# Issuing the adaLN weight rows of a hybrid layer from ScalarE's queue

## The chip, the cores and the metric

The kernel runs on one core of a Trainium2 chip. The core has five engines with instruction streams of their own: TensorE (PE, and PEld for its weight loads), VectorE (DVE), ScalarE (ACT), GpSimd (POOL) and the sync engine (SP). An engine takes its instructions in a fixed order; DMAs are instructions too, and occupy the queue of the engine that issues them, which first waits until the buffer to be filled is free. The transfer itself is done by 16 DMA engines that all queues share. The metric is the device time of one execution in microseconds.

## The reference

One layer works on x of 256 x 2048 (S = 256 positions) with a conditioning vector c of 2048, all in fp32:

```python
def _layer(x, c, w_ada, b_ada, ...):
    ada = (jax.nn.silu(c) @ w_ada + b_ada)[:, None, :]
    sh1, sc1, g1, sh2, sc2, g2, sh3, sc3, g3 = jnp.split(ada, N_ADA, axis=-1)
    h = _swiglu(_modulate(x, sh1, sc1), ffn1_w_in, ffn1_w_out)
    x = _layernorm(ALPHA * x + 0.5 * (1 + g1) * h, ln1_g, ln1_b)
    h = _token_mixer(_modulate(x, sh2, sc2), w_in, ..., w_out)
    x = _layernorm(ALPHA * x + (1 + g2) * h, ln2_g, ln2_b)
    h = _swiglu(_modulate(x, sh3, sc3), ffn2_w_in, ffn2_w_out)
    x = _layernorm(ALPHA * x + 0.5 * (1 + g3) * h, ln3_g, ln3_b)
    return x
```

The two feed-forward parts go from 2048 to 2 x 5632 and back. The token mixer has 8 attention heads with forget gates and 4 mLSTM heads. `w_ada` has 2048 x 18432 numbers, 151 MB, all used once, for a single vector: the product `silu(c) @ w_ada` gives nine vectors of 2048 features.

## The kernel before, in words

**Weights.** Every product with x or h has fp32 accuracy from three products of rounded numbers: high times high, low times high, high times low (`mm3`, L444 to L447). A weight tile of 1 MB (512 x 512) is loaded by SP into one of three buffers `raw` (`load_w`, L406); each half is then cast to its high part by ScalarE (L155) and its low part is the difference, taken by VectorE (L156). There are six buffers each for high and low parts, that is, three tiles. TensorE passes 24 products of 128 x 128 over 512 columns for a tile. A weight tile can be loaded as soon as the low part of the tile three before is taken.

**The ada rows.** The product with `w_ada` is done on VectorE: a row is a block of 128 x 1024 numbers (512 KB), and `acc += row * silu(c)` (L168 for the first row, L170 for the others) sums 16 of them into `acc` (or into part of `gate`), followed by a small TensorE product over the partitions that gives columns or gates. There are 288 such rows. Two buffers (`araw`) hold them: a row is asked for one ahead (`ask`, L188 to L192), so that its load waits until the sum of the row two earlier is done.

**Which rows, and when.** `AdaQueue` deals rows out to the weight tiles at a fixed rate (`R_F` 1.25 rows per tile in the first feed-forward part, 1.12 to 1.27 in the next ones, 1 and 0.7 in the last). The stages, with the times of the profile: the first features of x (shift and scale of the first norm, 512 features at a time) at the beginning, up to about 230 us, together with the first products (tiles `s`); the remainder of the first feed-forward input (`f1i`, 290 to 520), its output (`f1o`, to 760), the mixer (to 1160), the second feed-forward part (`gu`, `fh`, `f2i`, `f2o`, to the end). Rows last until 1500 us.

**The first features** are handled apart: the first 512 (`first_ada0`, L923) by 16 rows loaded by SP; the others (`first_ada(j)` for j = 1 to 3, L945 to L970) by 48 rows, three buffers (two `araw` and one `aw`), three of them on SP and 45 on GpSimd. After the last row of each, `first_columns` takes the columns (`cp`, L854; `scsh`, L856), which the next products need.

**The order.** The framework that turns the program into instruction streams has a planner of its own: it estimates times and sets the order on each engine by readiness and priority, so that a row's load stands in the queue where the planner puts it, not where it is written. At the changes of stage the order on VectorE and ScalarE is written out by hand. `tc.issue_after(ins)` keeps what is traced in its block behind `ins`, for instructions on the same engine as `ins`. One such block is in `load_mixer_smalls`, where three small loads wait behind the last row of `first_ada`:

```python
with tc.issue_after(pin_rows[0]):
    G_.dma_start(gbias[:, 0:8], fox_f_bias[0:1, :].to_broadcast([P, 8]))
    G_.dma_start(gbias[:, 8:12], mlstm_i_bias[0:1, :].to_broadcast([P, 4]))
    G_.dma_start(gbias[:, 12:16], mlstm_f_bias[0:1, :].to_broadcast([P, 4]))
```

In the code `SP`, `G_`, `S`, `V` and `PE` are the sync engine, GpSimd, ScalarE, VectorE and TensorE.

Of the kernel before, what the change touches and what calls it, by code (L numbers as in the profile page):

```python
# [14 lines left out]
P = 128  # L15
# [17 lines left out]
def layer_kernel(  # L33
# [8 lines left out]
    V, S, G_, PE, SP = nc.vector, nc.scalar, nc.gpsimd, nc.tensor, nc.sync  # L42
# [99 lines left out]
    pin_rows = [None]  # L142
# [20 lines left out]
    def pair_cols(v, j):  # L163
        return w_ada[0, :, v * D:(v + 2) * D].rearrange("k (v n) -> k v n", v=2)[:, :, j * 512:(j + 1) * 512]

    def ada_acc(acc, raw, k):
        if k == 0:
            V.tensor_scalar_mul(acc, raw, csil[:, k:k + 1])  # L168
        else:
            V.scalar_tensor_tensor(out=acc, in0=raw, scalar=csil[:, k:k + 1], in1=acc,  # L170
                                   op0=ALU.mult, op1=ALU.add)
# [14 lines left out]
    wanted, asked = [], []  # L186

    def ask():  # L188
        if wanted:
            shape, src, tag, k = wanted.pop(0)  # L190
            asked.append(ap.tile(shape, F32, tag="araw", bufs=2, name=f"ar{tag}_{k}"))
            SP.dma_start(asked[-1], src[k * P:(k + 1) * P])  # L192

    def ada_rows(acc):
        for k in range(KD):
            if not asked:
                ask()
            ada_acc(acc, asked.pop(0), k)
            ask()
            yield  # L200
# [140 lines left out]
    def modulate_both(v, j, rs, xT):  # L341
        xf = npool.tile([P, 4, T], F32, tag="xf", name=f"xf{ntag()}")
        n = xf.rearrange("p k t -> p (k t)").rearrange("p (a n) -> p a n", a=2)
        for a in range(2):
            S.activation(n[:, a, :], res[:, a, j * 512:(j + 1) * 512], AF.Identity, bias=rs[a][:, 1:2],
                         scale=rs[a][:, 0:1])
        yield
        tps = [aux_tile(f"tp{ntag()}") for _ in range(2)]
        for q in range(4):
            for a in range(2):  # L350
                PE.transpose(tps[q // 2][:, (2 * (q % 2) + a) * P:(2 * (q % 2) + a + 1) * P],
                             n[:, a, q * P:(q + 1) * P], ident)
        yield
        for q in range(4):
            k = 4 * j + q
            S.activation(xf[:, q, :], tps[q // 2][:, (q % 2) * T:(q % 2 + 1) * T], AF.Identity,
                         bias=scsh[:, v, k:k + 1], scale=scsh[:, v + 1, k:k + 1])
            hi, lo = (x[:, k, :] for x in xT[:2])
            cast = S.copy(hi, xf[:, q, :])  # L359
            yield  # L360
            x_cast[0] = cast.ins
            pin["x"] = V.tensor_tensor(out=lo, in0=xf[:, q, :], in1=hi.bitcast(F32), op=ALU.subtract).ins
            yield
# [483 lines left out]
    def first_columns(j, acc, mb):  # L847
        cps = aux_tile(f"cp{j}"), mm_tile(f"cq{j}")

        def column(q):  # L850
            cp = cps[q % 2][:, q:q + 2]
            qs = slice(q * P, (q + 1) * P)
            for v in range(2):
                PE.matmul(cp[:, v:v + 1], acc[:, v, qs], ones[:, 0:1], start=True, stop=True)  # L854
            k = 4 * j + q
            V.tensor_tensor(out=scsh[:, 0:2, k:k + 1], in0=cp.unsqueeze(2), in1=bcol[:, 0:2, k:k + 1], op=ALU.add)  # L856

        column(0)
        next(mb)
        column(1)  # L860
        next(mb)
        next(mb)
        column(2)
        next(mb)
        column(3)
        next(mb)
        for _ in mb:
            pass
# [77 lines left out]
    def first_ada(j):  # L946
        src = pair_cols(0, j)
        if j % 2:
            acc = ap.tile([P, 2, 512], F32, tag="acc", name=f"acc0_{j}")
        else:  # L950
            acc = gate[:, :1024].rearrange("p (v n) -> p v n", v=2)
        for k in range(KD):
            where, tag, n = (ep, "aw", 1) if k % 3 == 2 else (ap, "araw", 2)
            raw = where.tile([P, 2, 512], F32, tag=tag, bufs=n, name=f"ar0_{j}_{k}")
            pin_rows[0] = (SP if j == 1 and k < 3 else G_).dma_start(raw, src[k * P:(k + 1) * P]).ins
            if k < KD - 1:
                ada_acc(acc, raw, k)
            else:
                for b in range(2):
                    bs = slice(b * 256, (b + 1) * 256)  # L960
                    ada_acc(acc[:, :, bs], raw[:, :, bs], k)
            if k == 11:
                mb = modulate_both(0, j, rs0, xT)
            if k in (11, 13):
                next(mb)
            yield
        first_columns(j, acc, mb)
        yield
# [138 lines left out]
    for j in range(4):  # L1107
        fa = first_ada(j + 1) if j < 3 else load_mixer_smalls()
        for i in range(NS):
            with ExitStack() as s:  # L1110
                if j == 0 and i in (1, 2):

                    s.enter_context(tc.issue_after(x_cast[0]))
                    s.enter_context(tc.issue_after(pin["x"]))
                first_in(j, i, ws if i + j == 0 else first_w(j, i))
            for _ in range((2 * (j > 0), 1 + 2 * (j == 0), 2, 1, 2, 2, 1, 2, 1, 2, 1, 0)[i] if j < 3
                           else i not in (4, 9, 11)):
                with pinned():
                    next(fa, 0)
            if j == 3 and i > 2:  # L1120
                pump(R_F)
# [692 lines left out]
```

## Time and profile before

| | |
|---|---|
| three runs | 1854.41, 1858.54, 1861.12 us |
| median | 1858.54 us |
| profiled execution | 1855.95 us, span of the instructions 1854.2 us |
| TensorE busy | 1820.5 us of the span |
| VectorE busy | 1452.9 us |
| ScalarE busy | 926.3 us |
| GpSimd busy | 61.7 us |
| mean granted TensorE clock | 0.997 of full speed |
| transferred | 510.44 MB, mean 275 GB/s |

The profile names each group by source line, engine, operation and tile. PEld is the loading of the stationary operand, which overlaps the products. A letter q behind an engine (SPq, ACTq) is its sequencer, where waits for semaphores and DMA issues take place; these are not counted as busy time. In lists of waits the three numbers are total, times and longest.

### The profile page before, as it was taken

Reading aid. Unit: us, or ns where it says so; the run is one execution under the profiler, and the core shown is the slowest. Engines: PE = TensorE matmul, PEld = TensorE weight load, DVE = VectorE, ACT = ScalarE, POOL = GpSimd, SP = SyncE. Lnnn points to the kernel's source line nnn. Section 1 sums busy time; section 2 is a strip of 40 time slices with the busy share of each in tenths; the row PEclk is TensorE's granted clock in tenths of the full one; section 3 lists DMA queues with packets and bytes.
Section 4 is the critical chain, followed back from the end, with each engine's and each line's share of the span. In section 5 each row is a group of like instructions: output and inputs, shape, how many; then the busy total and the mean of one; then the engine's idle time right before and its main releaser. Section 6 shows DMA issues by size and latency. Waiting matters only on the chain.

```text
span 1854.2 us, 25052 instructions
## 1 busy us (share of the span) xinstructions
PE 1820.5 (98%) x9577; PEld 1599.3 (86%) x9577; DVE 1452.9 (78%) x1787; ACT 926.3 (50%) x1332; POOL 61.7 (3%) x92
## 2 busy tenths in 40 slices
PE   7999999999999999999999999999999999999997
PEld 4888888888888888699999887888889999988887
DVE  6889989877787787788889888787997766564655
ACT  3554455443554344755666645555465444554441
POOL 1211100000000000000000000000000000000000
PEclk9999999999999999999999999999999999999999
DMA  9989978988988898489979883998877876666663
GB/s 364 379 293 328 328 231 304 328 308 299 312 294 276 304 305 315 151 295 320 325 264 307 327 298 117 326 347 287 303 255 254 274 233 201 205 204 201 203 202 144
DMA packets 242927, 510.44 MB, mean 275 GB/s; under 512 B 10834, under 2 KB 52466, under 8 KB 241784
## 3 DMA queue, kind: packets, MB, share of 16 engines
q1 hardware_dynamic: 234696, 477.90, 74.7%
q0 software_dynamic: 8112, 30.95, 4.8%
q8 instruction: 75, 1.23, 0.3%
q14 instruction: 44, 0.36, 0.0%
HBM read 506.71 MB, written 2.10 MB: 274 GB/s over the span
## 4 chain that ended last, share of the span: by engine, by line
PE 56%; DVE 1%; issue 1%; ACT 0%; DMA 0%; POOL 0%; DVEq 0%; ACTq 0%; POOLq 0%; SPq 0%
PE gu_f L450 8%; PE o_f L446 4%; PE o_f L445 4%; PE o_f L447 4%; PE gu_f L451 4%; PE fh L446 4%; PE fh L447 4%; PE fh L445 4%; PE o_mx L445 1%; PE o_mx L446 1%; PE o_mx L447 1%; PE b_mv L445 1%; PE b_fv L445 1%; PE pr_m L445 1%; PE b_mv L446 1%; PE b_fv L446 1%
## 5 line engine op out<-in xcount | busy, mean ns | idle before, releaser
L170 DVE SCALAR_TENSOR_TENSOR acc<-ar,csil,acc 128x1024 f32<-128x1024 f32 (+1 forms) x167 | 211.7, 1269 | 65.8 <-DMA ar<-in_w_ada_dram 65.4
L450 PE MATMUL gu_f<-x_f,hi_f2i 128*128 128x512 f32 x640 | 210.0, 382 | 0.0
L451 PE MATMUL gu_f<-x_f,lo_f2i 128*128 128x256 f32 x640 | 174.5, 273 | 0.0
L156 DVE TENSOR_TENSOR lo_f2o<-raw_f2o,hi_f2o 128x1024 fp32r<-128x1024 f32 x86 | 105.2, 1224 | 86.7 <-ACT hi_f2o L155 86.6
L155 ACT CAST hi_s<-raw_s 128x1024 fp32r<-128x1024 f32 x96 | 99.1, 1047 | 117.4 <-PE s L447 64.8
L155 ACT CAST hi_f1o<-raw_f1o 128x1024 fp32r<-128x1024 f32 x86 | 88.4, 1047 | 120.6 <-PE o_f L447 63.3
L155 ACT CAST hi_f2o<-raw_f2o 128x1024 fp32r<-128x1024 f32 x86 | 90.1, 1047 | 115.6 <-PE o_f L447 107.0
L446 PE MATMUL s<-lo_s,x_f 128*128 128x512 f32 x384 | 146.2, 381 | 1.2 <-DVE lo_s L156 1.1
L445 PE MATMUL s<-hi_s,x_f 128*128 128x512 f32 x384 | 146.4, 383 | 0.2 <-ACT x_f L359 0.2
L447 PE MATMUL s<-hi_s,x_f 128*128 128x512 f32 x384 | 145.5, 379 | 0.0
L156 DVE TENSOR_TENSOR lo_f2i<-raw_f2i,hi_f2i 128x1024 fp32r<-128x1024 f32 x80 | 97.9, 1224 | 54.2 <-ACT hi_f2i L155 53.7
L450 PEld LDWEIGHTS gu_f<-x_f,hi_f2i 128*128 128x128 f32 x640 | 121.0, 189 | 16.8
L445 PE MATMUL o_f<-hi_f1o,hi 128*128 128x512 f32 x344 | 131.4, 382 | 3.1 <-DVE hT L1021 2.0
L447 PE MATMUL o_f<-hi_f1o,lo 128*128 128x512 f32 x344 | 131.0, 381 | 0.0
L446 PE MATMUL o_f<-lo_f1o,hi 128*128 128x512 f32 x344 | 131.0, 381 | 0.0
L155 ACT CAST hi_f1i<-raw_f1i 128x1024 fp32r<-128x1024 f32 x80 | 81.1, 1045 | 99.4 <-DMA raw_f1i<-in_ffn_w_in_dram 71.8
L170 DVE SCALAR_TENSOR_TENSOR gate<-ar,csil,gate 128x1024 f32<-128x1024 f32 (+1 forms) x94 | 117.5, 1251 | 16.3 <-DMA ar<-in_w_ada_dram 15.9
L156 DVE TENSOR_TENSOR lo_s<-raw_s,hi_s 128x1024 fp32r<-128x1024 f32 x96 | 115.9, 1220 | 14.8 <-ACT hi_s L155 14.8
L445 PE MATMUL o_f<-hi_f2o,hi 128*128 128x512 f32 x332 | 125.8, 379 | 0.0
L446 PE MATMUL o_f<-lo_f2o,hi 128*128 128x512 f32 x332 | 125.8, 379 | 0.0
L447 PE MATMUL o_f<-hi_f2o,lo 128*128 128x512 f32 x332 | 125.8, 379 | 0.0
L155 ACT CAST hi_fh<-raw_fh 128x1024 fp32r<-128x1024 f32 x80 | 82.4, 1048 | 81.3 <-DMA raw_fh<-in_ffn_w_in_dram 37.0
(447 smaller groups left out, 4830.7 us busy)
## 6 DMA issues: line engine op xcount, KB each, us to landing
ar<-in_w_ada_dram SPq DMA_DIRECT2D x230, 512.0 KB, 5.5
raw_s<-in_ffn_w_in_dram SPq DMA_DIRECT2D x47, 1024.0 KB, 7.6
raw_f1o<-in_ffn_w_out_dram SPq DMA_DIRECT2D x44, 1024.0 KB, 7.3
raw_f2o<-in_ffn_w_out_dram SPq DMA_DIRECT2D x44, 1024.0 KB, 5.0
raw_f1i<-in_ffn_w_in_dram SPq DMA_DIRECT2D x40, 1024.0 KB, 7.5
raw_fh<-in_ffn_w_in_dram SPq DMA_DIRECT2D x40, 1024.0 KB, 7.4
raw_f2i<-in_ffn_w_in_dram SPq DMA_DIRECT2D x40, 1024.0 KB, 5.8
ar<-in_w_ada_dram POOLq DMA_DIRECT2D x45, 512.0 KB, 6.3
```

The lines of the kernel that those rows point to most:

```text
L155: S.copy(hi, src)
L156: return V.tensor_tensor(out=lo, in0=src, in1=hi.bitcast(F32), op=ALU.subtract)
L170: V.scalar_tensor_tensor(out=acc, in0=raw, scalar=csil[:, k:k + 1], in1=acc, op0=ALU.mult, op1=ALU.add)
L445: PE.matmul(o, ah, bh, start=start, stop=False)
L446: PE.matmul(o, ah, bl, start=False, stop=False)
L447: PE.matmul(o, al, bh, start=False, stop=stop)
L450: PE.matmul(o, ah, x.rearrange("p s (a n) -> p s n a", a=2), start=start, stop=False)
L451: PE.matmul(o[:, T:], al, woven(x[:, 0]), start=False, stop=stop)
```

## The change

Two lines. The rows that `ask` loads (224 in the trace) go from SP's queue to ScalarE's, and the 45 rows of `first_ada` that GpSimd loaded do so too. The first 16 rows (`first_ada0`) and the three of j = 1 remain on SP. Nothing else is edited: buffers, rates and sums are the same.

```diff
@@ ask
             shape, src, tag, k = wanted.pop(0)
             asked.append(ap.tile(shape, F32, tag="araw", bufs=2, name=f"ar{tag}_{k}"))
-            SP.dma_start(asked[-1], src[k * P:(k + 1) * P])
+            S.dma_start(asked[-1], src[k * P:(k + 1) * P])
@@ first_ada
             where, tag, n = (ep, "aw", 1) if k % 3 == 2 else (ap, "araw", 2)
             raw = where.tile([P, 2, 512], F32, tag=tag, bufs=n, name=f"ar0_{j}_{k}")
-            pin_rows[0] = (SP if j == 1 and k < 3 else G_).dma_start(raw, src[k * P:(k + 1) * P]).ins
+            pin_rows[0] = (SP if j == 1 and k < 3 else S).dma_start(raw, src[k * P:(k + 1) * P]).ins
```

## The prediction

> **What bounds the kernel now.** I read the busy times first, then the table by stretches of time, then the waits, the sync engine's own waits, and last the timeline of the one stage in which the row loads touch the critical path. The time of the profiled execution is 1855.95 us for a span of 1854.2, 2.6 us below the median of the three runs (1858.54); the sum below is made against 1855.95, and 2.6 is added to compare with medians.
>
> ```profile
> PE 1820.5 (98%) x9577; PEld 1599.3 (86%) x9577; DVE 1452.9 (78%) x1787; ACT 926.3 (50%) x1332; POOL 61.7 (3%) x92
> ...
> 0.00:40.00 40.00, 29.30 (x110) 16.84 (x111) 24.02 (x55) 10.26 (x16) 2.81 (x11) 1.00 0.98 360
> 40.00:100.00 60.00, 56.94 (x272) 48.53 (x270) 48.16 (x45) 37.38 (x52) 11.77 (x16) 1.00 1.01 372
> 100.00:160.00 60.00, 60.00 (x286) 52.65 (x285) 55.53 (x62) 27.57 (x33) 10.14 (x14) 1.00 0.87 306
> 160.00:230.00 70.00, 69.06 (x335) 60.24 (x334) 67.05 (x80) 31.64 (x36) 13.60 (x20) 1.00 0.94 324
> ...
> 290.00:520.00 230.00, 228.34 (x1083) 199.22 (x1082) 179.15 (x172) 101.13 (x130) 1.08 (x2) 1.00 0.89 310
> 520.00:760.00 240.00, 235.93 (x1085) 204.32 (x1084) 192.78 (x217) 107.44 (x129) 3.34 (x5) 0.99 0.82 287
> 850.00:1060.00 210.00, 209.91 (x1590) 200.54 (x1589) 185.45 (x291) 130.00 (x249) 3.78 (x3) 1.00 0.88 305
> 1160.00:1310.00 150.00, 150.00 (x700) 131.31 (x699) 120.17 (x120) 82.14 (x105) 0.58 (x1) 1.00 0.91 319
> ```
>
> The columns after the length are busy PE, PEld, DVE, ACT and POOL, then the granted clock, the DMA share and GB/s. TensorE is the bound: 98% of the span. In the stretches in which rows are loaded it stands still 3.06 us (40 to 100), 0.94 (160 to 230), 1.66 (290 to 520) and 4.07 (520 to 760), together 9.73; in 850 to 1060 and 1160 to 1310 it hardly does (0.09 and 0.00). Nothing that is done to row loads can gain more than about these 9.73 us; what they can lose has no such limit. What ended those stops:
>
> ```profile
> PE o_f L445 <- DVE hT L1021: 2.0, 1, 2.0
> PE cp L854 <- DVE scsh L856: 1.9, 1, 1.9
> PE gu_f L446 <- DVE lo_f1i L156: 1.2, 2, 0.7
> PE o_f L445 <- DVE res L556: 1.1, 1, 1.1
> PE s L446 <- DVE lo_s L156: 1.1, 2, 0.8
> ```
>
> (Total, times, longest.) The low parts of weights (lo_f1i, lo_s) and the column product cp are late by a microsecond here and there; hT and res belong to the change of stage at 521 and 639 us and wait for no row.
>
> **The change part by part.** 224 rows of 512 KB go from SP to ScalarE (L192) and 45 from GpSimd to ScalarE (L955). The two buffers for rows, the order of the sums on VectorE and the bytes stay.
>
> ```profile
> L192 SPq DMA_DIRECT2D ar<-in_w_ada_dram x224: 327/367/500, 220.6 to 1499.1; - x112
> L955 POOL DMA_DIRECT2D ar<-in_w_ada_dram x45: 714/724/889, 43.0 to 217.4; - x45
> SPq L192 <- DVE acc L170: 233.3, 125, 7.0
> SPq L192 <- DMA ar<-in_w_ada_dram: 146.0, 90, 3.5
> SPq L192 <- DVE gate L170: 129.9, 64, 7.7
> ```
>
> *Issue time.* 269 x 0.37 = 99.5 us of ScalarE's queue, if an issue costs there what it costs on SP. ScalarE is busy 926.3 of 1854.2 us, so it has room: in 290 to 520, 50 rows take 18.5 of the 128.9 us it stands idle. By itself I take 0 for this; its cover is the lead of the casts over TensorE. Saved: 45 x 0.72 us on GpSimd, which nothing waits for, and 224 x 0.37 = 82 us on SP.
>
> *The waits.* Here lies the risk. On SP the row's issue waits for its buffer: 233.3 + 146.0 + 129.9 = 509 us over 224 rows, 2.3 us each, with only weight tiles behind it, which have three buffers. On ScalarE the same waiting instruction has casts (L155) behind it, and behind a cast VectorE's low part and TensorE. How much of the 2.3 us moves along depends on where the row will stand in ScalarE's order. Ends: nothing (the row stands where its buffer is free) and all of it. The stage of f1i, where ScalarE, VectorE and the row loads all wait:
>
> ```profile
> SPq L192 <- DVE acc L170: 45.8, 29, 4.8
> SPq L192 <- DMA ar<-in_w_ada_dram: 44.6, 28, 3.5
> SPq L192 <- DVE gate L170: 28.5, 15, 5.8
> ...
> ACT hi_f1i L155 <- DMA raw_f1i<-in_ffn_w_in_dram: 71.8, 24, 6.1
> DVE acc L170 <- DMA ar<-in_w_ada_dram: 21.1, 18, 2.8
> ...
> 419.77 5.68 SPq L192 DMA_DIRECT2D ar<-in_w_ada_dram  x2
> 425.54 0.42 SPq L406 DMA_DIRECT2D raw_f1i<-in_ffn_w_in_dram  x1
> ...
> 421.12 1.99 ACT L155 CAST hi_f1i<-raw_f1i 128x1024 fp32r<-128x1024 f32 x2 [5.51 <-DMA raw_f1i<-in_ffn_w_in_dram]
> ...
> 423.76 1.28 DVE L170 SCALAR_TENSOR_TENSOR acc<-ar,csil,acc 128x1024 f32<-128x1024 f32 x1 [1.75 <-DMA ar<-in_w_ada_dram]
> ...
> 462.22 0.62 ACT L155 CAST ahi<-acc 128x512 fp32r<-128x512 f32 x1 [8.45 <-DVE acc L170]
> ...
> 462.33 0.38 PE L445 MATMUL gu_f<-hi_f1i,x_f 128*128 128x512 f32 x1
> 463.38 0.48 PE L446 MATMUL gu_f<-lo_f1i,x_f 128*128 128x512 f32 x1 [0.67 <-DVE lo_f1i L156]
> ```
>
> (The first three are SP's waits in 290 to 520, the next two waits of the same stretch.) At 419.77 two rows hold SP until the second is issued just ahead of 425.45, and only then goes the weight tile out; ScalarE in turn waits 5.51 and then, from the same view, again for weights. That speaks for the change: a tile that leaves SP without a row ahead of it lands earlier. The last three rows price the danger: ScalarE, held 8.45 us for a sum on VectorE (from 453.77, two casts before it), leaves TensorE a step of 463.38 - 462.33 = 1.05 us instead of the 0.21 between neighbours (228.34 / 1083), 0.84 us lost. So a single hold costs TensorE what goes beyond about 7.6 us, and the short holds of a row (longest on SP here 5.8) cost nothing by themselves, only by adding up. What adds up: SP's whole wait would be 45.8 + 44.6 + 28.5 = 118.9 us, and with 18.5 of issue 137.4 against ScalarE's idle 128.9, 8.5 too much; the break-even is (128.9 - 18.5) / 50 = 2.2 us a row. I take the middle, about 1.2 us a row, since ScalarE reaches a row only after a cast that itself waits (24 of them waited 3 us each for weights) and finds the buffer freer than SP did: no loss from the adding up. Against the gain of at most 1.66 us stand a few thin places; I set this stage to +0.5, bounds -1.7 and +8.5.
>
> A rule that speaks against the change: the Trainium skill, "Perfetto Trace Analysis", section "DMA Instruction — HWDGE (DVE, Sync)", has the sequencer itself wait for the DMA's semaphore and stay taken until the descriptors are made, so a waiting row would shut ScalarE for all behind it. SP's rows agree for that queue (the 5.68 us above); none shows ScalarE's. By the rule with SP's whole waits the stage loses the 8.5 us, by the middle wait nothing.
>
> *First phase, 40 to 230 us.* The 45 rows come off GpSimd's queue:
>
> ```profile
> ACT hi_s L155 <- DMA raw_s<-in_ffn_w_in_dram: 20.7, 10, 3.6
> ...
> 51.72 0.72 POOL L955 DMA_DIRECT2D ar<-in_w_ada_dram  x1 [5.39 <-DVE acc L170]
> ...
> 50.13 1.28 DVE L170 SCALAR_TENSOR_TENSOR acc<-ar,csil,acc 128x1024 f32<-128x1024 f32 x1 [1.62 <-DMA ar<-in_w_ada_dram]
> ```
>
> The sum that frees the buffer ends at 51.41 and GpSimd starts at 51.72 for 0.72: 0.31 late and 0.35 longer than an issue of 0.37, so each row can leave 0.66 us sooner, as long as ScalarE is not inside a cast (1.05 us) at that moment, which costs 0.5 on the mean. That is even. In 40 to 100 the DMA engines are full (share 1.01), so landing is set by bytes; ScalarE has 60 - 37.4 = 22.6 us left, of which 16 rows take 5.9. Its waits of 20.7 us for raw_s lie in the same 22.6, so a row that holds it delays a cast only where the tile has landed. I take +0.5 (bounds -3.1, all of TensorE's idle time there, and +4: 16 rows with a hold of 0.25). For 100 to 230, with 28 and 38 us idle on ScalarE and VectorE at 93 and 96%, -0.3 (bounds -0.9 and +1): the sum on VectorE is the limit, and only the 0.94 us before the column product can be gained.
>
> *Later stages.* SP's waits before rows in 520 to 760 (the first two rows) and in 850 to 1060 (the other three):
>
> ```profile
> SPq L192 <- DVE acc L170: 58.7, 36, 7.0
> SPq L192 <- DMA ar<-in_w_ada_dram: 34.1, 20, 3.4
> ...
> SPq L192 <- DVE acc L170: 31.1, 13, 6.8
> SPq L192 <- DVE gate L170: 29.4, 17, 4.7
> SPq L192 <- DMA ar<-in_w_ada_dram: 29.3, 16, 3.4
> ```
>
> In 520 to 760, the out projection, they are 92.8 us, with 14.7 of issue for 40 rows, against 132.6 us idle on ScalarE: covered even in full. The 4.07 us of idle TensorE hang on hT and res. 0 (bounds -1, +3). In the mixer, 850 to 1060, they are 89.8 us, with 14.5 of issue for 44 rows 104.3, against 80.0 us idle on ScalarE: the break-even of (80.0 - 14.5) / 44 = 1.5 us a row is the lowest of all stages, yet TensorE has no gap now, so the middle of 2.0 and nothing stays under it. +0.5 (bounds 0, +10). In 1160 to 1310 ScalarE is idle 67.9 us of 150 for 29 rows, and TensorE loses nothing today; 0 with the rest (bounds 0, +2).
>
> *A load that comes free.* The three small loads of gate biases on GpSimd's queue are tied behind the last row of the first phase (L130, `pin_rows[0]`), an order that holds them only while that row is on GpSimd:
>
> ```profile
> 218.07 0.57 POOL L131 DMA_DIRECT2D gbias<-in_fox_f_bias_dram  x1
> ```
>
> With the row on ScalarE they can go out at the start, into 0 to 40 us, where the DMA share is 0.98 and TensorE has 10.7 us idle. Three issues of 0.57 at most make 1.7 us of GpSimd; I take +0.7 (0 to +1.5) for their packets among those of the first tiles.
>
> Sum: 0.7 + 0.5 - 0.3 + 0.5 + 0 + 0.5 + 0 = +1.9 on 1855.95: 1857.9, and with the 2.6 about 1860. 0.3% is 5.6 us, about what a measurement of this kernel can tell from no change; +1.9 is inside.
>
> **The rivals.** *ScalarE is held at the rows (slower).* Place: f1i and the mixer, where row, cast and sum form a ring: the row waits for a sum, the sum stands on VectorE behind a low part, the low part waits for a cast, the cast stands behind the row. It decides once the mean hold passes 2.2 us (f1i) or 1.5 us (mixer). At SP's whole wait: +8.5 in f1i, and 104.3 - 80.0 = 24.3 in the mixer, of which I take half, as these waits overlap ScalarE's own; with 0.7 + 0.5 that is +22: about 1880; at half that excess +11.5: 1870. For it: the 2.3 us mean wait on SP. Against: the 7.6 us of lead shown at 462.
>
> *Rows and weights no longer stand behind each other (faster).* It takes the 3.06 + 0.94 + 1.66 = 5.7 us of TensorE's stops, and perhaps one of the 4.07: 5.7 to 7.7, so 1851 to 1853 as a median. For it: 425.54 above. Against: only 1.66 us of stops in f1i come near a late tile, and DMA is at 0.87 to 1.01. The Trainium skill, "DMA: Bandwidth & Descriptors", section "Queues, rings and completion order", lets each DMA engine alternate between its queues by packets, by which a row would pass a tile in flight instead of following it; its section "Issuing engines are not separate DMA queues" grants only the issue time. No row here has rows and weights on two hardware queues.
>
> *The order hardly changes.* Rows placed on ScalarE where their buffers are long free: nothing held, but a row issued later makes VectorE wait (21.1 us in f1i now, up to 2.8 at once), within TensorE's lead: -1 to +2, indistinguishable from my forecast and counted with it.
>
> **How the numbers follow.** No measurable change 0.46; held ScalarE 0.34, of which a third beyond 1870; free queues 0.20. The range leaves out 0.1 at each end: 1850 (the free queues' lower end, a little below) to 1874. The likeliest case's own range is 1854 to 1865. Faster by over 0.3% needs all of the 5.7 us and takes the 0.20; slower 0.34; same 0.46.
>
> **What the profile of the changed kernel would show.** Rows as ACTq at L192 and L955, 0.37 us each, and waits of ACTq for acc and gate of L170: right if under 1.5 us a row, wrong above 2.2. SP's waits for weights alone; raw_f1i's issue right behind its lo_f1i; ScalarE's 71.8 us for raw_f1i shorter. TensorE's idle time by stretch within 2 us of that above. gbias within the first microseconds. What would make the forecast wrong: new stops of TensorE before lo_f1i in 290 to 520 or lo of the mixer in 850 to 1060, or an end of the stops before cp and lo_s.

## The result and the profile after

The changed kernel took 1885.75 us in the median (1884.89 to 1890.15) against 1856.92 for the kernel before in the same comparison: 1.0158 times as long, 95% interval 1.0136 to 1.0180, or 29 us slower. The prediction was 1860, in a range from 1850 to 1874. The profiled execution has a span of 1883.1 us, 28.9 more than before.

The line of busy times on the changed kernel's page:

```profile
PE 1829.8 (97%) x9577; PEld 1604.4 (85%) x9577; DVE 1453.7 (77%) x1787; ACT 927.6 (49%) x1332; POOL 29.0 (2%) x47
```

The same kernel's table by stretches (length; busy PE, PEld, DVE, ACT, POOL, with instructions; granted clock, DMA share, GB/s):

```profile
0.00:40.00 40.00, 27.29 (x101) 15.22 (x102) 22.77 (x53) 8.26 (x13) 4.58 (x14) 1.00 0.98 343
40.00:100.00 60.00, 56.30 (x263) 48.02 (x261) 47.54 (x43) 36.60 (x49) 0.00 (x0) 1.00 0.96 343
100.00:160.00 60.00, 56.89 (x267) 49.47 (x268) 48.64 (x57) 27.71 (x34) 0.00 (x0) 0.97 0.87 300
...
290.00:520.00 230.00, 226.26 (x1072) 196.93 (x1071) 179.42 (x176) 103.04 (x135) 1.08 (x2) 1.00 0.89 309
520.00:760.00 240.00, 232.63 (x1061) 201.42 (x1060) 189.51 (x193) 104.57 (x117) 1.06 (x2) 0.99 0.83 288
760.00:850.00 90.00, 84.79 (x430) 68.14 (x429) 69.94 (x131) 53.77 (x108) 5.85 (x10) 0.98 0.64 221
850.00:1060.00 210.00, 206.01 (x1643) 199.16 (x1642) 175.56 (x267) 123.31 (x232) 3.76 (x3) 1.00 0.85 290
```

The line for 760 to 850 of the kernel before:

```profile
760.00:850.00 90.00, 88.38 (x544) 75.35 (x543) 72.90 (x123) 58.59 (x115) 3.57 (x8) 1.00 0.77 261
```

And what the changed kernel's TensorE waited for (total us, count, longest), without the waits of the first 10 us:

```profile
PE gu_f L446 <- DVE lo_f1i L156: 3.2, 3, 1.5
PE cp L854 <- DVE scsh L856: 3.1, 1, 3.1
PE o_f L445 <- DVE hT L1021: 3.0, 1, 3.0
PE s L446 <- DVE lo_s L156: 3.0, 3, 1.3
PE o_f L446 <- DVE lo_f1o L156: 2.8, 3, 2.2
PE pr_fb L447 <- DVE lo_fb L156: 2.6, 1, 2.6
PE b_fv L445 <- ACT og L1564: 2.5, 1, 2.5
```

TensorE does the same 9577 products. It stands still 53.3 us of the span (1883.1 - 1829.8) instead of 33.7, and is busy 9.3 us longer for the same work. So 19.6 of the 28.9 us are stops and 9.3 are slower products (the last section says where most of these come from). The stops have grown in every stage with rows up to 1060 us, a little each time. Followed by the same product in both traces, the changed kernel is behind by 1.9 us at the first product of L925, by 9.8 at the last column product of the first phase (240.6 against 230.8), by 12.3 at the first product of f1o, 19.1 at its end, 27.8 at the mixer's tile fa and 28.7 from 1170 us to the end.

What the rows now do, first by the view of the line that loads them (issues with their time in ns, then the landings):

```profile
L192 ACTq DMA_DIRECT2D ar<-in_w_ada_dram x224: 334/374/386, 230.4 to 1527.8; - x112
DMA to landing us min/median/max: 3.5/5.5/8.7
```

Then by the waits of ScalarE and VectorE (total us, count, longest):

```profile
ACT hi_f1o L155 <- DVE acc L170: 50.4, 22, 6.2
ACT hi_f1i L155 <- DVE acc L170: 33.2, 14, 4.2
ACT hi_f1i L155 <- DVE gate L170: 16.3, 8, 3.2
ACT hi_f1i L155 <- DMA raw_f1i<-in_ffn_w_in_dram: 13.3, 7, 3.7
```

```profile
DVE acc L170 <- DMA ar<-in_w_ada_dram: 86.9, 59, 5.6
DVE gate L170 <- DMA ar<-in_w_ada_dram: 27.7, 18, 3.7
```

In the kernel before, VectorE waited less at rows, 15.9 us at `gate` and at `acc`:

```profile
DVE acc L170 <- DMA ar<-in_w_ada_dram: 65.4, 60, 2.8
```

A cast hi_f1o needs no sum `acc`. That it waits for one means that a row's load stands ahead of it on ScalarE and waits for its buffer. All such waits, those of `ahi` left out, are 187 us in 83 places; before there were none. The waits for raw_f1i have shrunk from 71.8 to 13.3 us. This looks like the rival of the held ScalarE, and the timeline of a long stop of f1o can be read that way too, in the changed kernel's rows of ScalarE, of VectorE and of TensorE, one after the other:

```profile
713.25 0.37 ACTq L192 DMA_DIRECT2D ar<-in_w_ada_dram  x1
713.74 1.05 ACT L155 CAST hi_f1o<-raw_f1o 128x1024 fp32r<-128x1024 f32 x1 [1.31 <-DVE acc L170]
719.49 0.37 ACTq L192 DMA_DIRECT2D ar<-in_w_ada_dram  x1
719.96 1.05 ACT L155 CAST hi_f1o<-raw_f1o 128x1024 fp32r<-128x1024 f32 x1 [5.18 <-DVE acc L170]
```

```profile
713.13 1.22 DVE L156 TENSOR_TENSOR lo_f1o<-raw_f1o,hi_f1o 128x1024 fp32r<-128x1024 f32 x1
718.17 1.28 DVE L170 SCALAR_TENSOR_TENSOR acc<-ar,csil,acc 128x1024 f32<-128x1024 f32 x1 [3.83 <-DMA ar<-in_w_ada_dram]
719.38 1.22 DVE L156 TENSOR_TENSOR lo_f1o<-raw_f1o,hi_f1o 128x1024 fp32r<-128x1024 f32 x1
```

```profile
718.06 0.38 PE L445 MATMUL o_f<-hi_f1o,hi 128*128 128x512 f32 x1
720.65 0.48 PE L446 MATMUL o_f<-lo_f1o,hi 128*128 128x512 f32 x1 [2.20 <-DVE lo_f1o L156]
```

The low part that TensorE waits for (719.38) belongs to the cast of 713.74, which was done at 714.79. It was ready to run 4.6 us earlier, but in VectorE's order a row's sum stands ahead of it, and that row landed only at 718.1. In the kernel before, the same low part (the 69th of f1o) and the next one stand ahead of that sum, the 149th of all row sums, which starts at 701.80:

```profile
699.07 2.35 DVE L156 TENSOR_TENSOR lo_f1o<-raw_f1o,hi_f1o 128x1024 fp32r<-128x1024 f32 x2
701.80 1.28 DVE L170 SCALAR_TENSOR_TENSOR acc<-ar,csil,acc 128x1024 f32<-128x1024 f32 x1 [0.37 <-DMA ar<-in_w_ada_dram]
```

In this stop it is VectorE that waits at the wrong instruction; ScalarE's hold of 5.18 us delays the next cast. The experiments take the two apart.

### The profile page after: what moved, and what is told of

Same layout as the page of the kernel before. It is cut to its first block, busy times and chain, and to the rows that moved or that the text cites. A ratio compares the mean times of both kernels' runs of the same rounds, so it can differ in the third digit from the quotient of the medians.

```text
span 1883.1 us, 25043 instructions
## 1 busy us (share of the span) xinstructions
PE 1829.8 (97%) x9577; PEld 1604.4 (85%) x9577; DVE 1453.7 (77%) x1787; ACT 927.6 (49%) x1332; POOL 29.0 (2%) x47
## 4 chain that ended last, share of the span: by engine, by line
PE 47%; DVE 5%; DMA 4%; issue 2%; ACT 2%; POOL 0%; ACTq 0%; DVEq 0%; POOLq 0%; SPq 0%
PE gu_f L450 7%; PE o_f L447 4%; PE o_f L445 4%; PE o_f L446 4%; PE gu_f L451 4%; PE fh L445 4%; PE fh L447 4%; PE fh L446 4%; DMA ar<-in_w_ada_dram 3%; PE b_fv L445 1%; DVE acc L170 1%; PE b_fv L446 1%; PE b_fv L447 1%; PE ge L793 1%; DVE gate L170 1%
## 5 line engine op out<-in xcount | busy, mean ns | idle before, releaser
L156 DVE TENSOR_TENSOR lo_f2o<-raw_f2o,hi_f2o 128x1024 fp32r<-128x1024 f32 x86 | 105.2, 1225 | 86.6 <-ACT hi_f2o L155 86.5
L446 PE MATMUL s<-lo_s,x_f 128*128 128x512 f32 x384 | 147.3, 384 | 3.0 <-DVE lo_s L156 3.0
L156 DVE TENSOR_TENSOR lo_f2i<-raw_f2i,hi_f2i 128x1024 fp32r<-128x1024 f32 x80 | 97.9, 1224 | 50.0 <-ACT hi_f2i L155 49.5
L446 PE MATMUL o_f<-lo_f1o,hi 128*128 128x512 f32 x344 | 131.9, 383 | 2.8 <-DVE lo_f1o L156 2.8
L156 DVE TENSOR_TENSOR lo_s<-raw_s,hi_s 128x1024 fp32r<-128x1024 f32 x96 | 115.8, 1221 | 15.3 <-ACT hi_s L155 15.2
L446 PE MATMUL o_f<-lo_f2o,hi 128*128 128x512 f32 x332 | 125.8, 379 | 0.0
L446 PE MATMUL gu_f<-lo_f1i,x_f 128*128 128x512 f32 x320 | 121.6, 380 | 3.2 <-DVE lo_f1i L156 3.2
```

What stands on the lines that cost most here:

```text
L156: return V.tensor_tensor(out=lo, in0=src, in1=hi.bitcast(F32), op=ALU.subtract)
L446: PE.matmul(o, ah, bl, start=False, stop=False)
```

## The experiments

Two counts are used below. The *hold* is the sum of ScalarE's waits, `ahi` left out, that a row's sum ended. The *place* is counted in the instruction order of the built programs, without any time: how many more rows' sums stand ahead of a low part on VectorE than in the kernel before, as a mean over the low parts of f1i / f1o / fv (fv is the mixer's first tile after 800 us). Moving the rows changes this place although no line on VectorE is edited. My reading, which no run shows, is that the planner expects a row on another queue than SP's sooner and so sets its sum further ahead. The table has the ratio to the kernel before in the same comparison, with its 95% interval.

| kernel | rows of L192 on | place f1i / f1o / fv | hold, us | ratio |
|---|---|---|---|---|
| late_rows_only | ScalarE | +0.21 / +0.21 / +0.71 | 190 | 1.0128 [1.0108, 1.0149] |
| gpsimd_rows | GpSimd | +0.20 / +0.21 / +0.46 | 5 | 1.0112 [1.0095, 1.0128] |
| issue_only | SP | 0 / 0 / -0.21 | 9 | 0.9992 [0.9981, 1.0003] |
| hold_only | SP | 0 / 0 / +0.08 | 149 | 1.0016 [0.9999, 1.0033] |
| eighth_row | 1/8 ScalarE | +0.09 / +0.12 / +0.33 | 118 | 1.0060 [1.0040, 1.0079] |
| half_row_each | 1/2 ScalarE | +0.21 / +0.26 / +0.62 | 164 | 1.0112 [1.0077, 1.0146] |
| sums_first | SP | +0.23 / +0.21 / +0.71 | 0 | 1.0052 [1.0032, 1.0072] |
| hold_and_sums_first | SP | +0.23 / +0.21 / +0.71 | 154 | 1.0071 [1.0044, 1.0098] |
| sp_waits_scalar | ScalarE | as late_rows_only | - | 1.0146 [1.0122, 1.0170] |
| sp_waits_gpsimd | GpSimd | +0.20 / +0.21 / +0.46 | - | 1.0114 [1.0078, 1.0150] |
| before_later | SP | -0.42 / -0.72 / -1.00 | - | 1.0001 [0.9986, 1.0016] |
| late_rows_later | ScalarE | -0.24 / -0.60 / -0.75 | - | 1.0105 [1.0086, 1.0124] |
| gpsimd_later | GpSimd | -0.24 / -0.60 / -0.79 | - | 1.0142 [1.0113, 1.0172] |
| late_rows_old_order | ScalarE | 0 but for two | 142 | 1.0168 [1.0140, 1.0196] |

**Which rows.** Each of the two lines alone.

```diff
 late_rows_only (on the kernel before)
-            SP.dma_start(asked[-1], src[k * P:(k + 1) * P])
+            S.dma_start(asked[-1], src[k * P:(k + 1) * P])
 first_rows_only (on the kernel before)
-            pin_rows[0] = (SP if j == 1 and k < 3 else G_).dma_start(raw, src[k * P:(k + 1) * P]).ins
+            pin_rows[0] = (SP if j == 1 and k < 3 else S).dma_start(raw, src[k * P:(k + 1) * P]).ins
```

> Only the 224 rows of L192 go to ScalarE; the 45 of L955 and with them the bias loads stay on GpSimd as before. In the changed kernel TensorE is 10.2 us behind the kernel before at the last column product of the first phase (237.4 against 227.2) and 28.8 behind at the end, so if the stages add up this one should come out 18 to 19 us slower than before, with its loss in 640 to 760 and 800 to 980. Theory H (ScalarE held at rows until a sum on VectorE frees the buffer): +15 to +20, and casts that wait for the sums of rows, about 200 us of them. A rival, that the loss of the first phase causes those later ones by shifting everything: below +5.

> Only the 45 rows of L955 go to ScalarE; the bias loads come free. By adding up: +8 to +12 us, of which about 2 lie before 35 us and the rest between 40 and 230, and nothing after 240. If what was lost in the first phase is caught up later: below +4.

The 224 rows alone: 1.0128, some 24 us. The 45 rows of the first phase: 1.0022 [1.0008, 1.0036], some 4 us. They add up to the change within their intervals. The first-phase rows cost less than I expected, as the rival had it: in that run's trace TensorE is 4.9 us behind at the last column product and 2.4 at the end.

**The freed bias loads.** The hold of the three small loads taken out of the kernel before, nothing else.

```diff
-        with tc.issue_after(pin_rows[0]):
-            G_.dma_start(gbias[:, 0:8], fox_f_bias[0:1, :].to_broadcast([P, 8]))
+        G_.dma_start(gbias[:, 0:8], fox_f_bias[0:1, :].to_broadcast([P, 8]))
 ...
```

> The kernel before without the hold of the three bias loads on GpSimd. Theory B (the freed loads make the first tiles late): the first product of L925 starts at about 11.2 us instead of 9.4, as in the changed kernel and in first_rows_only. Rival (the 1.9 us of the head come from ScalarE's rows): 9.4 us. No time is read from this one.

The first products on the row tiles, and with them the first bias loads where they are let go early, from the timelines of the kernel before, of biases_free and of the changed one, in this order:

```profile
9.48 4.04 PE L925 MATMUL row<-hT,csil 128*128 128x512 f32 x5 [6.64 <-DMA hT<-in_w_ada_dram]
```

```profile
11.66 2.05 PE L924 MATMUL row<-hT,csil 128*128 128x512 f32 x2 [8.79 <-DMA hT<-in_w_ada_dram]
...
1.84 0.71 POOL L130 DMA_DIRECT2D gbias<-in_fox_f_bias_dram  x1
2.55 0.55 POOL L131 DMA_DIRECT2D gbias<-in_mlstm_i_bias_dram  x1
```

```profile
11.33 2.05 PE L925 MATMUL row<-hT,csil 128*128 128x512 f32 x2 [8.61 <-DMA hT<-in_w_ada_dram]
...
1.84 0.71 POOL L131 DMA_DIRECT2D gbias<-in_fox_f_bias_dram  x1
```

So two of the three small loads, 6 KB, let go at 1.84 and 2.55 us, make the first product wait 1.9 to 2.2 us longer for its tile of 128 x 512, with or without rows on ScalarE (the third goes out at 9.9 us in both kernels). The cause of this delay in the head is shown. That all of it lasts to the end is not: biases_free was timed once, 1858.03 us against 1856.88 in the median for the kernel before, whose own runs differ by more.

**Is it ScalarE, and is it the issue?**

```diff
 gpsimd_rows (on the kernel before)
-            SP.dma_start(asked[-1], src[k * P:(k + 1) * P])
+            G_.dma_start(asked[-1], src[k * P:(k + 1) * P])
 issue_only: the row stays on SP, and behind it
+            spare_n[0] += 1
+            with tc.issue_after(pin_s[0]):      # the last cast traced
+                S.dma_start(spare[:, spare_n[0] % 8, :], src[k * P:(k + 1) * P, 0:2])
```

> The 224 rows of L192 go to GpSimd's queue instead, so that they leave the sync engine's queue as in the change but hold no engine that has other work. Theory H: no loss of the kind of the change, -4 to +4 us against before. Rival Q (rows and weights on two queues share the DMA engines so that one of them lands too late, whoever issues): +10 to +20, as in the change. Rival F (rows on SP delay the weights): -3 to -6.

> The rows stay on SP; ScalarE issues beside each of the 224 a small load of 128 x 2 numbers into a spare place that nothing reads, behind the last cast traced, with nothing to wait for. Theory H: within 3 us of before, since an issue alone of 0.37 us fits into ScalarE's idle time. Rival I (the issue time itself makes the casts late): +10 to +19.

224 more DMA issues on ScalarE cost nothing. The rows on GpSimd, which holds no engine that has other work, cost 1.12%, nearly what they cost on ScalarE. My theory H, the held ScalarE, expected -4 to +4 us there and falls as the main cause. (A row on GpSimd also starts 0.27 us later and takes 0.36 us longer to issue; no run takes that apart from the rest.) Rival Q expected this; the landings speak against it, though. The rows' loads in the kernel before, by the view of L192:

```profile
L192 SPq DMA_DIRECT2D ar<-in_w_ada_dram x224: 327/367/500, 220.6 to 1499.1; - x112
DMA to landing us min/median/max: 3.6/5.5/9.3
```

The median is 5.5 us as in the changed kernel. Rows issued 1 to 4 us behind a weight tile, between 290 and 1160 us, are those for which a shared queue should matter most. Where the profile tells their landing, it came after 6.35 us in the mean before (37 rows), 6.47 on ScalarE (37 rows of late_rows_only), 6.07 on GpSimd (89). Weight tiles land no later either: in f1i and f1o after 7.5 and 7.3 us in the median before, 7.4 and 7.0 in the changed kernel, 7.2 and 6.5 in gpsimd_rows. And on ScalarE a row starts 0.03 us after the sum that frees its buffer, in the median of every stage, as on SP; on GpSimd 0.30 us after. So in these medians and means rows are neither issued nor landed noticeably later on ScalarE.

**The hold alone.** The rows stay on SP; each row's buffer gets two more columns, and ScalarE loads these, so that it waits for the same buffer at each row.

```diff
 hold_only (on the kernel before)
-            asked.append(ap.tile(shape, F32, tag="araw", bufs=2, name=f"ar{tag}_{k}"))
-            SP.dma_start(asked[-1], src[k * P:(k + 1) * P])
+            whole = ap.tile([P, 1026], F32, tag="araw", bufs=2, name=f"ar{tag}_{k}")
+            row = whole[:, :1024]      # seen as shape
+            asked.append(row)
+            SP.dma_start(row, src[k * P:(k + 1) * P])
+            S.dma_start(whole[:, 1024:], src[k * P:(k + 1) * P, 0:2])
```

> Rows on SP as before, VectorE's order of sums and low parts as before but for two places; but each buffer for rows is 2 numbers wider, and ScalarE loads these 2 x 128 (nobody reads them) at each of the 224 rows. So ScalarE's queue waits at each row for the same buffer as in the change, without carrying the row. Theory H (ScalarE held): a third or more of the 23 us of late_rows_only, +7 to +20, with the stop before the sigmoid rows at 820 us (og) there. Theory O (order on VectorE alone): within 4 us of before.

Its ScalarE waits:

```profile
ACT hi_f1o L155 <- DVE acc L170: 46.5, 19, 3.8
ACT hi_f1i L155 <- DVE acc L170: 28.4, 13, 4.7
ACT hi_f1i L155 <- DVE gate L170: 20.9, 9, 4.4
```

ScalarE is held 149 us in 72 places, nearly as in the changed kernel, and the time is 1.0016 [0.9999, 1.0033]: at most 6 us, in the middle 3. With VectorE's order as before, a hold of this size costs little.

**The order alone.** `sums_first` keeps all queues of the kernel before and ties 53 low parts behind the row's sum that stands ahead of them in late_rows_only. `hold_and_sums_first` adds the two columns of hold_only.

```diff
 sums_first (on the kernel before)
+    sums_first = {'lo_s3_100': 'ar2_0_5', 'lo_f1i6_030': 'ar2_0_12', ...}   # 53 pairs
 ...
             with ExitStack() as s:
+                if f"lo_{name}{q}" in sums_first:
+                    s.enter_context(tc.issue_after(summed[sums_first[f"lo_{name}{q}"]]))
                 pin["w"] = split(raw[:, q * h:(q + 1) * h, :], hi, lo).ins
```

> The queues of the kernel before (rows on SP, GpSimd), but 53 low parts on VectorE are held behind the sum that stands ahead of them when the 224 rows are on ScalarE, so that VectorE's order of sums and low parts is that of late_rows_only but for three places. Theory O (the new order on VectorE, with a row's sum one or two places further ahead, is what costs; the queue itself costs little): at least half of the 20 to 23 us, so +10 to +23 against before, with stops of TensorE at lo_f1o near 700 us and at fv near 820. Rivals H (ScalarE held) and Q (shares of the DMA engines): within 4 us of before, since the rows are on SP.

> Both: VectorE's order as in sums_first, and ScalarE held as in hold_only, rows still on SP. If order and hold together are the cause and the queue that carries the row is none: +18 to +26 us against before, as late_rows_only (1.0128). If there is a third cause in the queue itself: below +14. Theory O alone: as sums_first, +6 to +13.

With not one DMA moved, the order alone costs 1.0052 [1.0032, 1.0072], 6 to 13 us. TensorE's waits in this run:

```profile
PE gu_f L503 <- DVE lo_f1i L210: 6.1, 4, 2.3
PE b_fv L503 <- DVE lo_fv L210: 3.9, 3, 2.8
PE o_f L503 <- DVE lo_f1o L210: 2.7, 2, 2.0
```

These are low parts (L503 and L210 are L446 and L156 there), in f1i, f1o and fv, where the places moved. Order and hold together give 1.0071 [1.0044, 1.0098], some 13 us. That is below the 18 to 26 us for order and hold as the whole cause, and inside both other forecasts (a third cause, below +14; the order alone, +6 to +13): of late_rows_only's 1.28% some 0.6% is still missing.

The stages don't match either. By TensorE's positions the order alone loses 8.2 us in f1i, 0.2 in f1o and 5.1 from there to the mixer's tile fa; the changed kernel loses 2.5, 6.8 and 8.7 there, late_rows_only 2.3, 3.2 and 11.8. These are single executions, in which a stage can differ by some us by chance (late_rows_only is already 4.3 us behind at the end of the first phase, where all its low parts but one keep their place). Still, the order alone loses most where the change loses least, so it isn't shown that the change loses its time in the way sums_first does.

**The other way.** Rows dealt out half a weight tile later, on each of the three queues; and, on ScalarE, single rows put off and low parts held until VectorE's order of sums and low parts is that of the kernel before.

```diff
 before_later, late_rows_later, gpsimd_later (load_w and AdaQueue.pump)
-            if q:
-                ada.half_step()
 ...
                 pin["w"] = split(raw[:, q * h:(q + 1) * h, :], hi, lo).ins
+            ada.half_step() if q else ada.late_row()    # late_row: the row that pump dealt out
 late_rows_old_order (on late_rows_only)
+            self.put_off = bool(self.owed >= 1 and low and low not in lows)   # low: the low part it must follow
+            if self.owed >= 1 and not self.put_off:
```

> The kernel before with every row of the ada queue dealt out half a weight tile later (behind that half's low part instead of ahead of it). Control for the next two: -3 to +5 us under each theory; more than +5 would mean that the rows are then missed at the ends of stages.

> late_rows_only with the same later dealing, which sets the sums behind the low parts again from the mixer on, and in part before (mean place -0.24 in f1i and -0.60 in f1o, where late_rows_only has +0.21). Theory O: at least half of the 23 us comes back, 1858 to 1869 us. Theory H: ScalarE is held at rows as before, 1874 to 1882. Theory Q: 1874 to 1882.

> gpsimd_rows with the same later dealing. Theory O: at least half of the 20 us comes back, 1858 to 1868 us. Theory Q (two queues sharing the DMA engines): 1872 to 1880. Theory H says nothing of this one, as no row is on ScalarE.

> The 224 rows on ScalarE as in late_rows_only, but rows are dealt out later, and low parts held, one by one, so that VectorE has the order of sums and low parts of the kernel before (all but two low parts). Theory O+H (the order on VectorE is most of the loss, ScalarE's hold a little): +2 to +9 us against before, so at least 14 of the 23 us come back. Rival C (something in the carrying queue beyond order and hold, which hold_and_sums_first with 0.71% against 1.28% left room for): +10 to +16. No theory of order at all: +20 or more.

Theory O, that this order is most of the loss, expected at least half of it back and missed three times: 1.0105, 1.0142 and 1.0168. The last is 31 us, what was forecast there for no effect of the order at all (+20 or more). Sums that come later do no harm on SP (1.0001), but they don't heal the other queues. In late_rows_old_order the forced places move other work too: 162 lines of VectorE's order and 24 of TensorE's differ from the kernel before (an instruction that moved counts twice), though the sums stand as before. No run has these other moves with the rows on SP, so they may hide what the order gave back; that stays open. So the places of sums against low parts can cost time by themselves (sums_first), but putting them back did not save it.

**The freed sync engine.** SP gets its waits back: the two spare columns are loaded by SP, the rows by ScalarE or GpSimd.

```diff
 sp_waits_scalar (hold_only with the two queues exchanged; sp_waits_gpsimd has G_)
+            S.dma_start(row, src[k * P:(k + 1) * P])
+            SP.dma_start(whole[:, 1024:], src[k * P:(k + 1) * P, 0:2])
```

> The 224 rows on ScalarE as in late_rows_only; each row's buffer is 2 numbers wider, and SP loads these 2 x 128 numbers (nobody reads them), so that SP waits at each row as before and weight tiles stand behind it. TensorE's and VectorE's orders are those of late_rows_only, instruction for instruction. Theory W (weight tiles that no longer wait behind rows leave too early and take the DMA engines from the rows): about half of the 23 us comes back, 1.003 to 1.009 of before. If the freed sync engine does not matter (order, hold and the row's own queue only): 1.010 to 1.015.

> The same with the rows on GpSimd, where nothing else is held: gpsimd_rows was 1.0112 of before. Theory W: 1.002 to 1.007, what the order on VectorE costs alone (sums_first, 1.0052) at most. If the freed sync engine does not matter: 1.009 to 1.014.

Nothing comes back (1.0146, 1.0114). That weight tiles leave SP without waiting behind rows is not what costs.

**By steps.** One row in two loads, one on each queue.

```diff
 half_row_each (eighth_row: 128 instead of 512)
+            S.dma_start(row[:, :512], rsrc[:, :512])
+            SP.dma_start(row[:, 512:], rsrc[:, 512:])
```

> Each of the 224 rows is loaded in two halves, 512 columns by ScalarE and 512 by SP into the same buffer. VectorE's order of sums and low parts is nearly that of late_rows_only (mean place +0.21 in f1i, +0.26 in f1o, +0.62 in fv against before), and ScalarE waits at each row. Order and hold: 1.006 to 1.013. If what counts is that the whole row is off SP: below 1.006.

> The same with 128 columns by ScalarE and 896 by SP: ScalarE waits at each row just as often, but the order moves half as far (+0.09 in f1i, +0.12 in f1o, +0.33 in fv). If the order makes the loss: between hold_only (1.0016, order unmoved) and half_row_each, 1.002 to 1.007. If ScalarE's hold makes it: as half_row_each.

With ScalarE waiting at each row in all three, the loss is 0.16% where the order stays (hold_only), 0.60% where it moves half as far, 1.12% where it moves as far as in late_rows_only. It does not go with the hold (149, 118 and 164 us), and an eighth of the bytes already brings half of the loss. In these three it goes with the order that the planner makes, of which the places of sums are the part that I counted. But the part of the row that ScalarE's queue carries grows along with it, and late_rows_old_order lost 1.68% with these places as before, so the three don't prove the order to be the cause.

## Why the prediction was wrong

The step that failed is a half sentence at the head of the change part by part: "The two buffers for rows, the order of the sums on VectorE and the bytes stay." Buffers and bytes stay; the order does not. The front of this document says that the planner sets it by its own estimates, and a load on another queue is another estimate. The sums moved ahead by up to two places in f1i, f1o and fv, and that by itself, with every queue as before, measured 1.0052, some 10 us. The prediction had no term for it. That the order is what makes the stops of the change is shown for single stops, not for the whole loss. Its third rival even had rows issued later on ScalarE; they are issued 0.03 us after the buffer frees, and what moved was VectorE.

The rows shown for f1i already had this cost in them, and the prediction took it for another. TensorE's step of 1.05 us at 463.38 waits for the low part that VectorE starts at 462.11. The cast of that low part, the 60th of f1i, was done at 453.77, before ScalarE's wait of 8.45 us began; two sums stood ahead of it on VectorE, at 458.79 and 460.90, and each waited over 0.8 us for its row. So this stop does not price a held ScalarE, and the "lead of 7.6 us" taken from it is no measurement of the lead.

- *Issue time, 0.* Right: issue_only, 0.9992.
- *The waits, the middle of 1.2 us a row.* The waits came about (187 us in 83 places; hold_only's 149 us are 0.7 us a row over 224), under the break-even of 2.2, which is what was named as a sign of being right. That they cost nothing to speak of was right: 1.0016 in the middle. The Trainium skill's "Perfetto Trace Analysis", section "DMA Instruction — HWDGE (DVE, Sync)", names the wait correctly for ScalarE as well: the sequencer stands at the row, and casts that need no sum wait for one. As a rule against the change it was worth 3 us here, not the 8.5 that I bounded for f1i.
- *First phase, +0.5 and -0.3, and the freed bias loads, +0.7.* The bias loads were the right mechanism and were mis-sized: 1.9 to 2.2 us, above the bound of 1.5. All first-phase rows with them cost 4 us, against a forecast of +0.9. In the changed kernel's trace the phase loses 9.8 us in all, in that of first_rows_only 4.9. (In 100 to 160 ScalarE stood idle 32.4 us, not 28, which is its busy time; nothing hangs on it.)
- *f1i +0.5, 520 to 760: 0, mixer +0.5.* By the positions in the changed kernel's trace these were 2.5 (12.3 - 9.8), 6.8 (19.1 - 12.3) and 8.7 (27.8 - 19.1) us. Half of the last, 4.4 us, is lost by 850 us, in a stretch that the list of stages with rows left out: 16 rows are loaded in 760 to 850, and TensorE's idle time there grew from 1.62 to 5.21 us. The out projection was "covered even in full", which counts ScalarE's waits only; the stop at 718 us is VectorE's wait at a row of 3.83 us with a ready low part behind it.
- *The rival of the held ScalarE* named the time best (1880), by a mechanism that measured 3 us alone. A rival that comes near the number is not shown by it.
- *Free queues (faster).* Its gain does not show: a row behind a weight tile lands in 6.1 to 6.5 us on the same queue or on another, and TensorE's stops grew. The Trainium skill's section "Issuing engines are not separate DMA queues" ("DMA: Bandwidth & Descriptors") grants only the issue time. The landings here agree, and 224 further issues on ScalarE changed nothing (0.9992).

What stays open: of the 1.28% of the 224 rows the counted order and the hold together make 0.71%, and the stages do not match. The rest could be the planner's remaining moves on VectorE and ScalarE (136 lines of VectorE's order differ between hold_and_sums_first and late_rows_only) or something in carrying the row on another queue that neither landing times nor issue times show. In gpsimd_rows TensorE's order is that of the kernel before and only 7 of ScalarE's instructions stand elsewhere, so there the rest is in VectorE's other moves or in the queue. No run here has the rows on ScalarE with the complete order of the kernel before, or on SP with the complete order after.

## What to carry to other kernels

Where a planner sets the order, a DMA moved to another queue is also an edit of every engine that consumes it: compare the instruction order of the two programs before reasoning about waits. A consumer that is set ahead of ready work can cost more than an engine that visibly waits: here the order alone measured 0.52% and ScalarE's hold alone 0.16%. When a stop is priced, look up when the awaited work became ready, and what its own engine did until it began. And an order that is tied to one engine (`issue_after`) falls silently when the instruction it hangs on changes engine: here two loads of 6 KB in all, freed into the head, made the first products 1.9 to 2.2 us late.

## What the runs showed of the hardware

Some stops cost more than their length. After the stop of f1o the timeline of TensorE goes on like this:

```profile
721.40 0.40 PE L446 MATMUL o_f<-lo_f1o,hi 128*128 128x512 f32 x1
721.62 0.61 PE L447 MATMUL o_f<-hi_f1o,lo 128*128 128x512 f32 x1
722.01 0.63 PE L445 MATMUL o_f<-hi_f1o,hi 128*128 128x512 f32 x1
...
724.57 0.62 PE L445 MATMUL o_f<-hi_f1o,hi 128*128 128x512 f32 x1
725.00 0.41 PE L446 MATMUL o_f<-lo_f1o,hi 128*128 128x512 f32 x1
```

The table by stretches has for these 4 us, columns as above:

```profile
721.00:725.00 4.00, 4.00 (x12) 3.21 (x11) 3.89 (x5) 1.51 (x4) 0.00 (x0) 0.58 0.73 206
```

One microsecond after a stop of 2.20 us the products come 0.43 us apart instead of 0.22, for 3.4 us; the granted clock of that stretch is 0.58. The records of the granted clock have five such half-speed stretches of 3.41 us between the first products and the end in the changed kernel (107, 172, 537, 722 and 831 us) and one before (525 us). At half speed 3.41 us do the work of 1.7, so four more are 6.8 of the 9.3 us by which TensorE is busy longer.

The stops at these five places are 3.11, 1.34, 2.97, 2.20 and 2.53 us long, and the slow stretch starts between 0.5 us before and 1.7 us after the stop's end. The length alone does not decide: a stop of 2.59 us in the same kernel, at 959 us, has no slow stretch behind it, and neither have two of about 1.55 us. So this trace gives no length up to which a stop is safe.
